# A decoder layer on eight cores: token-major residual, engines ordered by a list scheduler, and the two token mixers run side by side

## The chip, the cores and the metric

One Trainium2 chip, eight cores (two dies of four: cores 0 to 3 and 4 to 7). Each core runs the whole program on one batch element of 2048 tokens; nothing passes between the cores. The time is the device time of the slowest core, in microseconds (us). Some executions of any kernel here fall into a second, slower state, in which the cores of one die show a lower granted TensorE clock than the others. Those runs are marked slow.

Engines are named as in the profile: PE is TensorE's matmuls, PEld its weight loads, DVE VectorE, ACT ScalarE, POOL GpSimd, SP the queue that issues plain transfers.

## The reference, cut to what matters

```python
x = x + 0.5 * swiglu(rmsnorm(x), w1, w3, w2)            # D 1024, inner width 2816
h = rmsnorm(x)
u = h @ w_in                                            # q | k | v | ret gate | lru x | lru gate
# mixer A: retention, 4 heads (dk 128, dv 256), chunks of 128
ret   = retention_chunkwise(rotary(q), rotary(k), v)    # scan over 16 chunks
y_ret = (silu(g_ret) * head_groupnorm(ret)) @ w_ret_o
# mixer B: causal conv of 4 taps and a gated linear recurrence (RG-LRU), width 1024
xc = conv(x_lru)
r, i = sigmoid(xc @ w_rgate + b), sigmoid(xc @ w_igate + b)   # 8 blocks of 128
a  = exp(-8 * r * softplus(-lam))
h_t = a_t * h_{t-1} + sqrt(1 - a_t**2) * i_t * xc_t           # over time
y_lru = (h_t * gelu(g_lru)) @ w_lru_o
gates = sigmoid(h @ w_branch_gate + b)
x = x + (gates[:D] * y_ret + gates[D:] * y_lru) @ w_out
x = x + cross_attention(rmsnorm(x), rmsnorm(mem))       # 4 heads, 256 memory tokens
x = x + 0.5 * swiglu(rmsnorm(x), ...)
return rmsnorm(x)
```

The two mixers need only `h`, not each other. That is what the change uses.

## The kernel before

Operations are recorded in program order with what they read and write; each engine keeps that order, and semaphores are placed from the dependences. The mixers are two functions, called one after the other:

```python
lru_branch()
retention_branch()
mixer_tail()                     # merge projections, gates, output projection
```

The LRU works in units of one 128-channel block and half of the time axis (16 units). Every array has two sets, one for each half:

```python
def Bb(u):
    cc, hf = divmod(u, 2)
    S = sets[hf]
    # ... (tt = ii * tt on VectorE)
    if hf == 0:
        P.add("dve", lambda e: e.tensor_tensor_scan(hl.ap, ra.ap, tt_.ap, 0.0, ALU.mult, ALU.add), ...)
        P.add("dve", lambda e: e.tensor_copy(small[:, 24:25], hl.ap[:, TH - 1:TH]), reads=hl.hs, writes=[hcar])
    else:
        P.add("dve", lambda e: e.tensor_tensor_scan(hl.ap, ra.ap, tt_.ap, small[:, 24:25], ALU.mult, ALU.add), ...)
    P.add("pool", lambda e: e.tensor_tensor(BT[cc].ap[...], hl.ap, gg.ap, ALU.mult), ...)

A(0)
A2(0)
for u in range(NU):              # A: projections and conv; A2: gates; Bk_: exponentials; Bb: scan
    if u + 1 < NU:
        A(u + 1)
    Bk_(u)
    if u + 1 < NU:
        A2(u + 1)
    Bb(u)
```

In the merge, one weight tile serves four token blocks, so all eight PSUM banks fill before the first is emptied:

```python
for k in range(KC):
    for tb in range(NTB):
        ins = e.matmul(banks[bb[tb]][:, :], wt_[:, k, :], rhs_list(k, tb), start=(k == 0), stop=(k == KC - 1))
```

The softmax here doesn't subtract the row's maximum and nothing guards it: scores larger than these inputs give would overflow.

## Time and profile before

| | before |
|---|---|
| median (range) of 4 runs | 2755.9 us (2751.8 to 2759.6) |
| profiled core | core 3, 2769.7 us (an execution of its own) |
| TensorE busy, first feed-forward | 463 of 479 us, granted clock 0.98 |
| LRU alone, retention alone | 338 and 491 us, clock 0.67 and 0.78 |
| merge | 331 us |

The slices, windows, chain and groups behind this table are in the prediction, with what is to be seen in each. One reading to keep in mind: the window table gives, for each stretch of time, each engine's busy us with the number of instructions in brackets, then the granted TensorE clock as a share of full speed, the busy share of the DMA engines and their GB/s.

### The profile page before, as it was taken

What the parts mean: (1) busy time and instruction counts of PE and PEld (TensorE: products, weight loads), DVE (VectorE), ACT (ScalarE), POOL (GpSimd) and SP (SyncE); (2) the same over time, 40 slices, a digit from 0 to 9 for tenths busy, and PEclk for the clock granted to TensorE, in tenths of its full rate; (3) what the DMA queues carried; (4) which work ended last, traced back from release to release, by engine and by line L of the source; (5) the groups of instructions that cost most, each with busy time, mean ns of one, the idle gap of its engine ahead of it and who ended that gap; (6) DMA issues with size and microseconds to landing.
All of it is one profiled execution on the core that took longest, in us unless ns stands there. A gap on an engine that the chain in (4) does not pass through costs nothing.

```text
span 2769.7 us, 26087 instructions; the slowest of 8 cores (2732.2 to 2769.7 us)
## 1 busy us (share of the span) xinstructions
PE 2034.4 (73%) x8717; PEld 899.3 (32%) x8717; DVE 801.2 (29%) x1491; ACT 760.2 (27%) x1566; POOL 412.3 (15%) x441
## 2 busy tenths in 40 slices
PE   2599999965445545757576678877489699999993
PEld 2244444421111212323233233323234244444442
DVE  1313233143333352323233111112412423132333
ACT  1310100125677632333325111110323410101014
POOL 0000000001222234434343312210000000000000
PEclk9799999977667667878688888888799799999995
DMA  8022212051010033030300423333231202132103
GB/s 190 0 33 36 39 20 42 16 149 12 8 16 8 8 31 31 1 31 1 31 1 1 40 21 31 31 127 64 56 59 21 48 0 47 22 58 38 20 1 122
DMA packets 120851, 104.48 MB, mean 38 GB/s; under 512 B 78496, under 2 KB 103184, under 8 KB 118672
## 3 DMA queue, kind: packets, MB, share of 16 engines
q0 software_dynamic: 112880, 66.59, 18.1%
q1 hardware_dynamic: 7840, 36.24, 3.6%
q8 instruction: 71, 1.16, 0.2%
q14 instruction: 60, 0.49, 0.1%
HBM read 152.63 MB, written 16.78 MB: 61 GB/s over the span
## 4 chain that ended last, share of the span: by engine, by line
PE 69%; ACT 12%; DVE 6%; DMA 5%; issue 5%; POOL 2%; ACTq 0%; DVEq 0%; POOLq 0%; SPq 0%
PE bank L428 22%; PE bank L454 11%; PE bank L1181 10%; PE bank L1029 5%; PE bank L808 5%; PE bank L995 3%; PE bank L689 2%; ACT R L363 2%; PE bank L1214 2%; PE bank L614 2%; PE bank L370 2%; DMA ring<-w_in 2%; PE bank L844 1%; DVE R L499 1%; DMA R<-x 1%
## 5 line engine op out<-in xcount | busy, mean ns | idle before, releaser
L428 PE MATMUL bank<-R,ring 128*128 128x512 bf16 x2816 | 613.5, 381 | 14.3 <-DVE R L382 14.3
L428 PEld LDWEIGHTS bank<-R,ring 128*128 128x128 bf16 x2816 | 276.4, 98 | 351.3 <-issue 22.1
L454 PE MATMUL bank<-R,ring 128*128 128x512 bf16 x1408 | 313.6, 386 | 24.6 <-DVE R L437 24.6
L1181 PE MATMUL bank<-R,ring 128*128 128x512 bf16 x1024 | 263.1, 425 | 62.5 <-DVE R L1191 31.2
L434 ACT ACTIVATE R<-bank 128x512 f32<-128x512 f32 x176 | 90.9, 604 | 750.3 <-PE bank L428 750.3
L437 DVE TENSOR_TENSOR R<-bank,R 128x512 bf16<-128x512 f32 x176 | 109.2, 682 | 509.7 <-PE bank L428 509.7
L459 DVE SCALAR_TENSOR_TENSOR R<-bank,R 128x512 f32<-128x512 f32 x256 | 158.9, 682 | 178.8 <-PE bank L454 178.8
L454 PEld LDWEIGHTS bank<-R,ring 128*128 128x128 bf16 x1408 | 139.3, 99 | 198.9 <-issue 39.6
L1181 PEld LDWEIGHTS bank<-R,ring 128*128 128x128 bf16 x1024 | 108.4, 107 | 217.0 <-issue 122.8
L280 POOL DMA_DIRECT2D ring<-ffn_w x24 | 20.9, 874 | 1037.5 <-PE bank L428 611.1
L1029 PE MATMUL bank<-ring,R 128*128 128x512 bf16 x512 | 166.0, 483 | 0.1
L844 PE MATMUL bank<-R,wgate 128*128 128x512 bf16 x64 | 29.8, 621 | 175.5 <-ACT R L837 175.5
L995 PE MATMUL bank<-R,ring 128*128 128x512 bf16 x512 | 127.9, 417 | 28.9 <-DMA ring<-w_in 27.3
L808 PE MATMUL bank<-R,ring 128*128 128x512 bf16 x512 | 142.1, 447 | 0.0
L370 PE MATMUL bank<-R,onesb 128*128 128x512 bf16 x128 | 53.2, 591 | 95.8 <-ACT R L363 95.8
L829 DVE SCALAR_TENSOR_TENSOR R<-R,pc 128x1024 f32<-128x1024 f32 x48 | 61.6, 1284 | 191.0 <-ACT R L825 187.7
L1067 PE MATMUL bank<-R 128*128 128x256 bf16 x64 | 18.8, 294 | 121.8 <-ACT R L1062 116.5
L382 DVE SCALAR_TENSOR_TENSOR R<-R,pc,bank 128x512 bf16<-128x512 f32 x128 | 85.7, 741 | 72.4 <-ACT bank L379 72.4
L363 ACT ACTIVATE R<-R 128x512 bf16<-128x512 f32 x128 | 68.8, 618 | 76.0 <-DVE R L1219 76.0
L995 PEld LDWEIGHTS bank<-R,ring 128*128 128x128 bf16 x512 | 53.4, 105 | 102.4 <-issue 61.5
L808 PEld LDWEIGHTS bank<-R,ring 128*128 128x128 bf16 x512 | 58.0, 113 | 86.4 <-issue 66.0
L1029 PEld LDWEIGHTS bank<-ring,R 128*128 128x128 bf16 x512 | 59.7, 117 | 75.5 <-issue 47.9
(190 smaller groups left out, 2025.1 us busy)
## 6 DMA issues: line engine op xcount, KB each, us to landing
ring<-ffn_w POOLq DMA_DIRECT2D x12, 1536.0 KB, 12.7
ring<-ffn_w POOLq DMA_DIRECT2D x12, 1280.0 KB, 10.1
R<-x SPq DMA_DIRECT2D x16, 512.0 KB
park<-R SPq DMA_DIRECT2D x8, 1024.0 KB
R<-park SPq DMA_DIRECT2D x8, 1024.0 KB
out<-R SPq DMA_DIRECT2D x16, 512.0 KB
ring<-w_in POOLq DMA_DIRECT2D x24, 256.0 KB, 4.4
ring<-w_in POOLq DMA_DIRECT2D x8, 512.0 KB, 6.3
```

The source lines that it names most:

```text
L363: P.add("act", lambda e, c=c, tb=tb: e.activation(sq[c].ap, xT[(c, tb)].ap, AF.Square), reads=xT[(c, tb)].hs, writes=sq[c].hs)
L370: ins = e.matmul(banks[b][:, :], onesb[:, :], sq[c].ap, start=(c == 0), stop=(c == KC - 1))
L382: P.add("dve", lambda e, c=c, tb=tb, b=b: e.scalar_tensor_tensor(hT[(c, tb)].ap, xT[(c, tb)].ap, pcol(gname, c), banks[b][:, :], ALU.mult, ...
L428: ins = e.matmul(banks[bb[tb]][:, :], wtile[:, k, m * 128:(m + 1) * 128], hT[(k, tb)].ap, start=(k == 0), stop=(k == KC - 1))
L434: P.add("act", lambda e, tb=tb, ba=ba: e.activation(ssb[tb].ap, banks[ba[tb]][:, :], AF.Silu), reads=[hbk[ba[tb]]], writes=ssb[tb].hs)
L437: P.add("dve", lambda e, tb=tb, bb_=bb_, m=m: e.tensor_tensor(hid[(m, tb)].ap, banks[bb_[tb]][:, :], ssb[tb].ap, ALU.mult), reads=[hbk[bb_ ...
L454: ins = e.matmul(banks[bb[tb]][:, :], w2t[:, m, oc * 128:(oc + 1) * 128], hid[(m, tb)].ap, start=(m == 0), stop=(m == G - 1))
L459: P.add("dve", lambda e, tb=tb, bb=bb, oc=oc: e.scalar_tensor_tensor(xT[(oc, tb)].ap, banks[bb[tb]][:, :], 0.5, xT[(oc, tb)].ap, ALU.mult, ...
L808: ins = e.matmul(banks[bb[j]][:, :], wl_t[:, k, r, :], hT[(k, tbs[j])].ap, start=(k == 0), stop=(k == KC - 1))
L995: ins = e.matmul(banks[b][:, :], wt_[:, k, :], hT[(k, tb)].ap, start=(k == 0), stop=(k == KC - 1))
L1029: ins = e.matmul(banks[b][:, :], hT_all.ap[:, k, cols], wvg_t[:, k, :, :].rearrange("p r f -> p (r f)"), start=(k == 0), stop=(k == KC - 1))
L1181: ins = e.matmul(banks[bb[tb]][:, :], wt_[:, k, :], rhs_list(k, tb), start=(k == 0), stop=(k == KC - 1))
```

## The change

The intent: fill TensorE between the two feed-forward blocks. The residual is kept token-major (norms become row operations), the retention state is summed in PSUM, the memory projections are folded into the query and output weights, and LRU units and retention steps are emitted in turn. A list scheduler then lays every engine's instructions out from assumed durations. The core of the diff, cut:

```diff
-        if stage not in (23, 25, 26):
-            lru_branch()
-        retention_branch()
-        mixer_tail()
+        ret_load(0)
+        unit = lru_units()
+        ret_load(1)
+        step = ret_steps()
+        for s in range(16):
+            unit(s)
+            step(s // 8, s % 8)
+        tail()
 ...
+TAB_NS = 1283.0
+TAB_HOLD = 1200.0
 ...
+            if e == "act":
+                for (k, c, op) in a:
+                    pen = TAB_NS + TAB_HOLD if (op.tab is not None and tab[0] is not None and tab[0] not in op.tab) else 0.0
+                    cand = (t + pen, k, c, op)
 ...
+            xc = XC.v((u % 2) * 1024, 1024)
+            xcb = XCB.v()
+            tr = TR.v((u % 2) * 1024, 1024)
+            ti = TI.v()
+            mu = MU.v()
+            gg = GG.v((u % 2) * 1024, 1024)
 ...
-                P.add("dve", lambda e: e.tensor_copy(small[:, 24:25], hl.ap[:, TH - 1:TH]), reads=hl.hs, writes=[hcar])
+            prev = XC.v(((u + 1) % 2) * 1024 + 1023, 1)
 ...
+                dve(lambda e: e.tensor_tensor_scan(xc.ap, tr.ap, mu.ap, prev.ap, ALU.mult, ALU.add),
+                    tr.hs + mu.hs + prev.hs, xc.hs, 1024, 2.1)
 ...
-                    for k in range(KC):
-                        for tb in range(NTB):
-                            ins = e.matmul(banks[bb[tb]][:, :], wt_[:, k, :], rhs_list(k, tb), start=(k == 0), stop=(k == KC - 1))
+                    mm_group(banks[by][:, :], by, [(w.ap[:, 2 * br, k, :], sv[k].ap) for k in range(KC)], w.hs + hs)
+                    bg = bk.next()
+                    mm_group(banks[bg][:, :], bg, [(w.ap[:, 2 * br + 1, k, :], hT(tb, k).ap) for k in range(KC)], w.hs + hhs(tb))
```

TI, MU and XCB have one buffer each.

## The prediction

> **What bounds the kernel now.** I read the page's slices first, then cut the span into its stages by busy time and clock, then the chain that ended last, then the groups of instructions. Core 3, profiled at 2769.7 us, is the slowest of eight; the cores lie within 1.4% and no die lags, so this is a fast run.
>
> ```profile
> PE   2599999965445545757576678877489699999993
> ACT  1310100125677632333325111110323410101014
> PEclk9799999977667667878688888888799799999995
> ```
>
> These are tenths in 40 slices. TensorE is full in the two feed-forward blocks (slices 3 to 8 and 33 to 39) and at 4 to 8 tenths between them, where its granted clock is lower too. ScalarE leads only in the recurrent-unit stage.
>
> ```profile
> core 3: us, PE busy (x) PEld busy (x) DVE busy (x) ACT busy (x) POOL busy (x), PEclk, DMA share, GB/s
> 113.00:592.00 479.00, 463.45 (x2112) 207.91 (x2112) 134.26 (x219) 46.73 (x89) 7.82 (x9) 0.98 0.21 42
> 647.00:985.00 338.00, 161.46 (x544) 61.66 (x544) 116.03 (x86) 239.30 (x273) 79.72 (x42) 0.67 0.10 10
> 1045.00:1536.00 491.00, 313.43 (x1356) 140.05 (x1354) 145.38 (x560) 176.29 (x638) 206.28 (x271) 0.78 0.14 14
> 1536.00:1867.00 331.00, 263.46 (x1026) 108.49 (x1026) 39.72 (x64) 40.48 (x67) 65.31 (x63) 0.84 0.33 50
> ```
>
> In order: first feed-forward, the LRU branch alone, the retention branch alone, the merge projections. The same table gives the rest: start and first norm 113 us, mixer norm 55, rotary tables and first weights 60, output projection with the return of the residual 79, attention norm and memory keys and values 74, attention 164, norm 37, second feed-forward 477, transposes and store 72. Together 2770. Only 956 us are feed-forward; the other 1814 us hold about half of all matmuls.
>
> ```profile
> 244.53 82.89 PE bank L428 x384
> 1640.62 16.72 PE bank L1181 x64
> 1869.04 16.93 DMA ring<-w_out
> ```
>
> From the chain of waits (start, length, work). 82.89/384 = 0.216 us for a full-width matmul at full clock: this is my unit. The merge projections take 16.72/64 = 0.261 each, because every block of 64 follows a wait of about 4 us for VectorE to free banks and starts slow. The third line is a weight load that nothing covers.
>
> ```profile
> L459 DVE SCALAR_TENSOR_TENSOR R<-bank,R 128x512 f32<-128x512 f32 x256 | 158.9, 682 | 178.8 <-PE bank L454 178.8
> L829 DVE SCALAR_TENSOR_TENSOR R<-R,pc 128x1024 f32<-128x1024 f32 x48 | 61.6, 1284 | 191.0 <-ACT R L825 187.7
> L860 ACT ACT_TABLE_LOAD x16 | 20.5, 1283 | 0.3
> L862 ACT ACTIVATE R<-R,small 128x1024 f32<-128x1024 f32 x16 | 18.4, 1149 | 1.5
> PE bank L844 <- ACT R L837: 175.5, 16, 11.2
> ```
>
> These are prices (mean ns after the bar) and, last, the wait table's verdict on the LRU stage: TensorE stands 175.5 us of 338 behind one ScalarE instruction. The retention stage has the same shape with shorter waits.
>
> **What the Trainium skill says.** "TensorE: Matmul & The Clock Gate", Part 1, has a cold array at half clock until some 3.4 us of sustained work, N/1.2 against N/2.4 + 2.5 ns per matmul: 427 and 216 ns at 512 columns. The trace agrees: after a gap, weight loads of the merge projections are 0.43 us apart for about 14 matmuls, later 0.21. The same part warns of a limiter at 13/16 clock once three cores of a die run dense matmuls. The trace disagrees for the feed-forward (0.96 to 1.00 on all eight cores over stretches of 40 to 90 us), but 0.262 us spacing, which is 13/16, does show after the slow start of some LRU blocks. "ScalarE: Activation LUTs", What ACT_TABLE_LOAD costs, gives 1283 ns; the trace has 1283. Its section on table sets advises grouping by set; the kernel before loads three tables per LRU unit (48 in all).
>
> **The change, part by part.** Weights, head count and mathematics stay; layout, order and overlap change. I counted the built program's instructions and read their order on each engine. I price them with the durations above.
>
> *Start.* Ten small parameter loads one after another, f32 transposes and four ones-matmul norms (113 us) give way to a token-major norm (Square with accumulation, one scale, eight bf16 transposes per tile). TensorE's order has nearly all 16 tiles' transposes ahead of the dense part, so it waits for the whole of x. Before, 3 x 1.5 MB of bf16 weights, 9.4 MB of f32 read, arrived in 36 us and x alone at 8.4 MB in 25 us, say 260 to 335 GB/s. Here 8.9 MB share that with weights: about 58 us, and 5 for the last norm: 63, or 50 saved.
>
> *First feed-forward.* Its 2112 matmuls are the same: 456 us. Added inside are the memory keys, values and their folding into the query and output weights (192 half-width and 32 full-width matmuls, 28 us), 8 us of transposes for the next norm, and my estimate of 20 us for side loads that come late and for VectorE, which in the last group has two residual updates (0.68 each), a 1.28 scaling and half of a 1.0 copy per 2.2 us of matmuls. I put 512 against 479, but the 55 us norm after it goes.
>
> *Mixer.* The shifted q and k weights fall away (256 matmuls), state lives in PSUM, LRU and retention run together. TensorE at full clock: 576 + 256 + 512 full-width matmuls = 1344 x 0.216 = 290, small ones (256 at 128 columns, 184 at 256) 35: 325 us. ScalarE: an LRU unit is four copies or gelus (0.60), four gates (0.69), four 1024-wide passes (about 1.2): 10.0 us, x16 = 160; a retention step 6.8, x16 = 109; table switches, 22 in the built order, 28: 297. VectorE: LRU 8.25 x 16 = 132, rotary 96 x 0.69 = 66, masks and per-chunk statistics and scaling 103: 301. So three engines are nearly level, and perfect overlap would give some 330. But the order on TensorE shows that retention is served first: after its last matmul six of the 16 LRU units are still to come. Hence two parts. While both run (10 units, all of retention): TensorE 78 + 166 + 35 = 279, VectorE 251, ScalarE 222; at 85% TensorE occupancy 328. Then six units alone, ScalarE-bound: 10.0 + two table loads 2.6 + 2 for single buffers = 14.5 each: 87. With 10 for filling: 425 against 338 + 60 + 491 = 889.
>
> *Merge and output.* 1024 x 0.216 = 221 + 3, as banks now turn over per 16 matmuls, 3.5 us, against 0.69 + 0.68 of evacuation: 107 saved. Output 256 x 0.216 = 55 + 7 transposes + 3, the residual's reload running beside it: 65 against 79 + the norm part of 74.
>
> *Attention.* Query and output projections go into the folded matrices: 256 + 32 + 256 = 544 matmuls instead of 672: 118 + 7 transposes + 5 = 130, against 164 + 37, the memory part having left.
>
> *Second feed-forward, end.* 456 + 9 = 465. The last tile is already token-major: square, scale, 0.5 MB store, about 14 against 72.
>
> Sum: 63 + 512 + 425 + 224 + 65 + 130 + 465 + 14 = 1898. I predict 1905.
>
> **Rivals.**
> - *The clock limiter becomes the bound.* Weights now change at every matmul and the span has hardly a pause[...]. For: the 0.262 us spacing in LRU blocks. Against: retention's q/k projections, which already change weights each time, run at 29.7 us for 128, slow start included. If everything dense went to 13/16, 1400 us x 0.23 = 322 more: about 2230. I give it one in eight.
> - *ScalarE and the LRU chain hold the mixer.* The static order was made with assumed durations; TensorE, in order, may sit behind a late gate. Then the mixer is nearer 500 and the whole 1980. For: one pass costs DVE, POOL, PE and ACT in turn, and several buffers are single. Against: retention fills the gaps.
> - *Late side loads in the first feed-forward.* Sixteen memory jobs reuse two weight slots, each a 0.5 MB load that the trace lands in 4 to 6 us; a 3 us stall each would make 50 us: 1940.
> - *Everything overlaps as ordered*, 85% becomes 95%, and stalls vanish: about 1840.
>
> **Range and chances.** Downward I see 60 us, upward 80 from stalls and more from the clock, so 1840 to 2020. More than 840 us of the saving comes from idle time that is visible in the profile, and even the limiter case is 19% faster; being within 2% or slower would need a fault that I can't see: 0.98, 0.01, 0.01.
>
> **What would show it.** Feed-forward blocks of about 500 and 465 us at clock near 1.0, with 0.216 us per matmul (a 0.26 spacing there means the limiter); mixer near 425, of which the last 80 to 90 with TensorE under 60% and two table loads per unit; merge and output at 285 without 4 us gaps; no stage of norms; first dense matmul near 63 us. The prediction is wrong if the mixer exceeds 500, if the granted clock in the feed-forwards is near 0.8, or if TensorE waits for loads in the first one for over 40 us.

## The result, and the profile after

| | before | after |
|---|---|---|
| median of 4 runs | 2755.9 us | 2069.3 us |
| range | 2751.8 to 2759.6 | 2068.5 to 2070.0, and one slow run of 2249.5 |
| ratio of the fast runs | | 0.7509 (95%: 0.7497 to 0.7521) |

A ratio is the mean time of one kernel's fast runs over the mean of the other's fast runs in the same rounds, so it is not quite the ratio of the medians that are quoted.

The kernel is faster by a quarter, but 164 us longer than predicted, and outside the range of 1840 to 2020. The slices of the changed kernel, on its slowest core (core 5, 2068.1 us), in tenths:

```profile
PE   2599999999988877777554499999999999999997
ACT  3311121111335353535444431113544111111122
PEclk9699999999998989889766799999999999999999
```

TensorE is full from slice 3 on, except for slices 12 to 23: there it falls to 8, 7, 5 and 4 tenths and the clock falls with it. ScalarE stays at 3 to 5 tenths in the same place, so it isn't the full engine either. The stages from the first to the merge, as windows:

```profile
core 5: us, PE busy (x) PEld busy (x) DVE busy (x) ACT busy (x) POOL busy (x), PEclk, DMA share, GB/s
0.00:85.00 85.00, 21.56 (x150) 13.98 (x151) 28.55 (x60) 31.11 (x52) 25.33 (x45) 0.77 0.97 214
85.00:610.00 525.00, 501.92 (x2483) 235.04 (x2482) 218.03 (x345) 97.07 (x164) 49.41 (x92) 0.99 0.42 80
610.00:1036.00 426.00, 318.82 (x1550) 146.31 (x1547) 270.25 (x436) 202.32 (x333) 175.65 (x131) 0.88 0.09 24
1036.00:1183.00 147.00, 66.01 (x214) 23.38 (x214) 53.90 (x40) 69.17 (x80) 34.24 (x19) 0.67 0.04 7
1183.00:1406.00 223.00, 222.88 (x1027) 100.82 (x1028) 49.48 (x66) 52.35 (x72) 59.79 (x59) 0.99 0.28 49
```

In order: start, first feed-forward, mixers side by side, LRU units left over, merge. In the fourth line no engine is busy for half of the time: the engines wait for one another. Against the prediction's sum:

| stage | predicted | measured | difference |
|---|---|---|---|
| start | 63 | 85 | +22 |
| first feed-forward | 512 | 525 | +13 |
| mixers side by side (with 10 for filling) | 338 | 426 | +88 |
| LRU units left over | 87 | 147 | +60 |
| merge | 224 | 223 | -1 |
| output projection | 65 | 75 | +10 |
| attention | 130 | 129 | -1 |
| second feed-forward, end | 479 | 458 | -21 |
| sum | 1898 | 2068 | +170 |

Seven eighths of the miss is the mixer. From the chain of waits (start, length, work), the lines that answer to those of before:

```profile
1289.98 116.13 PE bank L505 x538
1406.14 19.39 DMA X<-park
1602.30 358.10 PE bank L505 x1658
```

In the merge 116.13/538 is 0.216 us a matmul where before had 0.261: the waits for banks are gone. The second line is the residual's reload, which the prediction had beside other work; TensorE is busy for 71.8 of the 75 us of the output stage all the same. The third is the second feed-forward at 358.10/1658 = 0.216 us. From the groups (line, engine, operation, tiles, count; busy us, mean ns of one; idle time before it):

```profile
L737 DVE SCALAR_TENSOR_TENSOR X<-bank,X 128x512 f32<-128x512 f32 x256 | 176.2, 691 | 111.6 <-PE bank L505 111.3
L521 ACT ACT_TABLE_LOAD x27 | 34.6, 1283 | 39.4 <-PE bank L505 30.7 <-DMA X<-x 8.4
```

Residual updates and table loads cost what before's cost (682 and 1283 ns). These prices were right; VectorE's work in the mixer, 343 us busy against 301 priced, was underpriced, and e5 below shows one reason. What was wrong in the main is in the wait table of the stretch 1036 to 1183 (engine, line, what it waited for; us in all, times, longest):

```profile
PE bank L505 <- POOL XCB L939: 57.7, 6, 20.4
PE bank L505 <- ACT TI L521: 17.9, 3, 17.5
PE bank L505 <- ACT TR L521: 14.1, 10, 4.6
```

Six waits of up to 20 us for XCB, the bf16 copy of the conv's result. Selected lines of the timeline around the longest of them (start, length, engine, line, operation, tiles; in brackets the idle time before it and what ended it):

```profile
1084.64 0.60 ACT L521 ACTIVATE XL<-bank 128x512 f32<-128x512 f32 x1 [1.91 <-PE bank L505]
1094.99 2.34 POOL L958 TENSOR_TENSOR MU<-TI,MU 128x1024 f32<-128x1024 f32 x1 [12.15 <-ACT MU L521]
1097.43 2.35 DVE L963 TENSOR_TENSOR_SCAN XC<-TR,XC,MU 128x1024 f32<-128x1024 f32 x1 [16.80 <-POOL MU L958]
1099.89 2.92 DVE L933 TENSOR_SCALAR XC<-XL,pc 128x1024 f32<-128x1024 f32 x1
1107.12 1.04 POOL L939 CAST XCB<-XC 128x1024 bf16<-128x1024 f32 x1 [4.85 <-DVE XC L936]
1108.30 1.01 PE L505 MATMUL bank<-XCB,wgate 128*128 128x512 bf16 x2 [20.36 <-POOL XCB L939]
```

The input of the next unit's conv (XL) is complete at 1085.24, but the conv (L933) starts at 1099.89, right after the scan (L963): the scan reads the old state from the array that the conv is to overwrite. VectorE stands idle for 16.80 us before the scan, and TensorE for 20.36 us. Two units take 1058.6 to 1112.6, 54 us.

The start's 22 us have at least two parts. Selected lines of its timeline, on the same core (JUNK<-X and JUNK<-MST are the sums of squares of a tile of x and of a memory tile, HB<-X the scaling of a tile of x before its transposes):

```profile
68.73 1.06 ACT L521 ACTIVATE JUNK<-X 128x1024 bf16<-128x1024 f32 x1 [2.35 <-DMA X<-x]
73.94 3.16 PE L505 MATMUL bank<-hT,W_45 128*128 128x512 bf16 x8
81.06 1.06 ACT L521 ACTIVATE JUNK<-MST 128x1024 bf16<-128x1024 f32 x1 [8.07 <-DMA MST<-mem]
82.31 0.15 DVE L641 TENSOR_SCALAR stat<-stat 128x1 f32<-128x1 f32 x1 [8.39 <-ACT JUNK L521]
83.08 1.28 DVE L650 SCALAR_TENSOR_TENSOR HB<-X,stat,ROW 128x1024 bf16<-128x1024 f32 x1
```

The last tile of x has landed by 68.73, against 58 in the prediction. But its scaling stands in VectorE's queue behind the statistics of the first memory tile, which lands only at 81; so it runs at 83.08, and its transposes at 84.51. This is queue order again: a tile for a side job holds the main path for some 7 us (an estimate: the x tile before it took 8.8 us from its sum of squares at 64.32 to its transposes at 73.13).

### The profile page after: what moved, and what is told of

Same layout as the page of the kernel before. It is cut to its first block, busy times and chain, and to the rows that moved or that the text cites. A ratio compares the mean times of both kernels' runs of the same rounds, so it can differ in the third digit from the quotient of the medians.

```text
span 2068.1 us, 24090 instructions; the slowest of 8 cores (2053.9 to 2068.1 us)
## 1 busy us (share of the span) xinstructions
PE 1776.2 (86%) x8584; PEld 815.4 (39%) x8584; DVE 904.4 (44%) x1354; ACT 615.8 (30%) x964; POOL 395.7 (19%) x435
## 4 chain that ended last, share of the span: by engine, by line
PE 70%; DVE 8%; DMA 6%; ACT 6%; issue 5%; POOL 2%; SPq 2%; DVEq 0%; ACTq 0%; POOLq 0%
PE bank L505 68%; DMA MST<-mem 2%; SPq L531 2%; ACT MU L521 2%; DVE XC L936 1%; ACT TR L521 1%; DMA XW<-w_xo 1%; POOL MU L958 1%; ACT L521 1%; DVE XC L933 1%; DMA X<-park 1%; PE bank L658 1%; DVE XC L963 1%; DMA XW<-w_xqT 1%; DMA rope<-RT 1%
## 5 line engine op out<-in xcount | busy, mean ns | idle before, releaser
L505 PE MATMUL bank<-hT,W_45 128*128 128x512 bf16 x2816 | 626.4, 382 | 2.3 <-ACT STMP L521 2.3
L505 PEld LDWEIGHTS bank<-hT,W_45 128*128 128x128 bf16 x2816 | 277.0, 99 | 333.4 <-issue 12.5
L505 PE MATMUL bank<-W_46,HID 128*128 128x512 bf16 x1408 | 314.2, 379 | 3.2 <-DVE stat L641 1.8
L719 DVE TENSOR_TENSOR HID<-bank,STMP 128x512 bf16<-128x512 f32 x176 | 121.7, 691 | 440.8 <-PE bank L505 439.1
L521 ACT ACTIVATE STMP<-bank 128x512 f32<-128x512 f32 x176 | 104.8, 596 | 686.0 <-PE bank L505 685.9
L737 DVE SCALAR_TENSOR_TENSOR X<-bank,X 128x512 f32<-128x512 f32 x256 | 176.2, 691 | 111.6 <-PE bank L505 111.3
L505 PEld LDWEIGHTS bank<-W_46,HID 128*128 128x128 bf16 x1408 | 131.8, 97 | 174.2 <-issue 29.6
L505 PE MATMUL bank<-hT,LW 128*128 128x512 bf16 x512 | 128.1, 412 | 22.9 <-ACT TI L521 22.6
L505 PE MATMUL bank<-hT,TW 128*128 128x512 bf16 x512 | 121.9, 382 | 0.0
L505 PE MATMUL bank<-RW_76,hT 128*128 128x512 bf16 x256 | 72.3, 437 | 22.4 <-DVE T_87 L1000 13.5
L505 PE MATMUL bank<-RW_75,hT 128*128 128x512 bf16 x256 | 69.4, 421 | 21.9 <-DVE T_87 L1000 10.4
L534 POOL DMA_DIRECT2D W_45<-f_w x44 | 24.4, 555 | 327.9 <-PE bank L505 327.4
```

The lines of the kernel that those rows point to most:

```text
L505: ins = e.matmul(out_ap, l, r, start=(start and i == 0), stop=(stop and i == n - 1), skip_group_check=skip)
L521: P.add("act", lambda e: e.activation(out, in_, func, **kw), reads=reads, writes=writes, cost=act_cost(n, nap), tab=tab)
L534: P.add("pool", lambda e: e.dma_start(out=out, in_=in_), reads=reads, writes=writes, cost=900, dma=nbytes)
L719: dve(lambda e: e.tensor_tensor(hd.ap, banks[b3][:, :], s.ap, ALU.mult), [hbk[b3]] + s.hs, hd.hs, TB)
L737: dve(lambda e, b=b, xv=xv: e.scalar_tensor_tensor(xv.ap, banks[b][:, :], 0.5, xv.ap, ALU.mult, ALU.add), [hbk[b]] + xv.hs, xv.hs, 512)
```

## The experiments

Two times mark the mixer in every run: the first LRU projection matmul and the first matmul of h with a merge weight. In the changed kernel these are 586.8 and 1183.3, so 596.5 us. The stretch begins inside the last 20 us of the first feed-forward; on this yardstick the prediction's 425 us are about 448. In all the full kernels the part from the first output-projection matmul to the end takes 659 to 663 us and the merge 220 to 231 (250 on the core of e2 whose clock was low in it, 223 on others), so nearly all that moves is start and mixer. The five jobs (e1 to e4, e5 to e8, e9 to e12, e13 to e16, e17 and e18) each ran the kernel before again, with medians of 2758 to 2773 us; across jobs it is the ratios that are to be compared.

| run | fast runs, us | ratio to before (95%) | mixer, us | clock in the mixer | longest TensorE wait there, us |
|---|---|---|---|---|---|
| changed kernel | 2068.5 to 2070.0 | 0.7509 (0.7497 to 0.7521) | 596.5 | 0.83 | 20.4 |
| e1 carry cell | 2007.5 to 2015.6 | 0.7291 (0.7272 to 0.7310) | 536.2 | 0.88 | 17.5 |
| e2 table hold 0 | 1997.9 to 2020.1 | 0.7244 (0.7227 to 0.7261) | 526.5 | 0.86 | 8.8 |
| e3 both | 1937.0 to 1940.6 | 0.7025 (0.7011 to 0.7040) | 463.6 | 0.97 | 3.4 |
| e4 start | 2041.8 and 2058.2 | 0.7429 (0.7383 to 0.7475) | 597.5 | 0.84 | 20.7 |
| e5 = e3, products on VectorE | 1940.4 to 1954.1 | 0.7058 (0.7009 to 0.7107) | 464.8 | 0.90 | 4.7 |
| e6 = e3, second MU | 1909.2 to 1912.2 | 0.6927 (0.6908 to 0.6947) | 438.5 | 0.96 | 3.1 |
| e7 = e3, LRU two ahead | 1996.7 and 1997.5 | 0.7239 (0.7213 to 0.7265) | 525.3 | 0.89 | 4.0 |
| e8 = e3 and e4 | 1932.8 to 1934.9 | 0.7010 (0.6991 to 0.7029) | 463.9 | 0.97 | 2.7 |
| e9 = e6, second rotary pair | 1945.9 to 1951.6 | 0.7057 (0.7020 to 0.7094) | 475.3 | 0.93 | 6.1 |
| e13 = e6's buffers, e3's order | 1938.5 to 1942.4 | 0.7036 (0.7018 to 0.7053) | 457.9 | 0.98 | 3.2 |
| e14 = e9's buffers, e6's order | 1895.3 to 1901.7 | 0.6881 (0.6864 to 0.6899) | 425.4 | 0.96 | 3.2 |
| e15 = e3, second TI, second rotary pair | 1907.8 to 1912.1 | 0.6923 (0.6907 to 0.6938) | 432.9 | 0.95 | 3.8 |
| e16 = e6 and e4 | 1876.3 to 1882.7 | 0.6811 (0.6794 to 0.6829) | 435.7 | 0.95 | 3.6 |
| e17 = e1 in the changed kernel's order | 2064.2 to 2068.0 | 0.7482 (0.7465 to 0.7499) | 592.2 | 0.83 | 20.3 |
| e18 = e14's buffers, e16's order | 1868.4 to 1872.0 | 0.6773 (0.6744 to 0.6802) | 426.1 | 0.97 | 2.9 |

All of these give correct results. e10 to e12 are wrong on purpose and stand further down.

### e1, e2, e3: the carry and the table hold

The theory: the scan's read of the other XC buffer ties the units in pairs, and the table hold puts the LRU's exponentials back so far that units are left over at the end. The rival: VectorE and GpSimd slow each other, and neither edit changes that.

```diff
 # e1
+    carry = fixed("carry", 16, F32)
-            prev = XC.v(((u + 1) % 2) * 1024 + 1023, 1)
+            prev = View(carry.ap[:, 0:1], carry.hs)
 ...     # after the first half's scan
+                dve(lambda e: e.tensor_copy(prev.ap, xc.ap[:, 1023:1024]), xc.hs, prev.hs, 1)
 # e2
-TAB_HOLD = 1200.0
+TAB_HOLD = 0.0
 # e3: both
```

> Edit: the scan's end value goes to a small cell of its own, so the next unit's convolution no longer waits for the scan that still reads the old buffer. Theory 'carry' (the unit pair is serial because of that buffer): after the last retention matmul the order now has 4 units instead of 6 to 7, and a pair takes about 36 us there instead of 54, so the stretch of LRU alone falls from 147 us to about 75 and the whole from 2069 to about 1995. Theory 'table hold' (units wait for the scheduler's reluctance to switch ScalarE's tables): exponentials are still held back, so no more than 20 us: about 2050. Theory 'contention' (VectorE and GpSimd slow each other): 2069, unchanged.

> Edit: one constant of the list scheduler, the extra 1200 ns that a table switch has to be worth, set to 0; the same instructions in another order. Theory 'table hold': the exponentials of a unit run some 20 to 40 us earlier, the LRU keeps pace with retention (the order has 1 unit of projections after the last retention matmul instead of 7), the stretch of LRU alone falls from 147 to 40 us, the shared part grows by about 20: near 1985. Theory 'carry': the pair stays serial, so the units cannot come faster than one per 27 us; 16 of them in 430 us just fit, so this too allows 1990 to 2030. Theory 'contention': 2069, or worse as more VectorE and GpSimd work falls into the shared part.

> Both edits. If the two causes are separate links of one chain, no LRU unit is left at the end (the order says so) and the mixer becomes the shared part alone, about 450 us instead of 573: 1945. If either alone is the cause, this equals the better of the two single edits within 10 us. If contention or the clock sets the shared part, it lengthens by what the units bring, some 60 us, and the gain stops at 2000.

Measured: the ratio falls from 0.7509 to 0.7291, 0.7244 and 0.7025, which is 60, 73 and 133 us of before's 2756. The two gains add, and nearly all of it is in the mixer: 60, 70 and 133 us shorter. By the medians e1 gained 57 us where its theory said 74, e2's 1999.6 us lie in the range of 'carry' (1990 to 2030) and 15 over the 1985 of 'table hold', and e3's 1939.7 are close to the 1945 expected. The rival theory of contention, for which e1 should have changed nothing, doesn't explain this part. Of the LRU units' projections, the built order of the changed kernel leaves 7 behind the last retention projection, e1's leaves 4, e2's 1, e3's none. Together the edits take away 133 of the 148 us by which the mixer had missed.

Part of this is clock. The same mixer matmuls keep TensorE busy for 405.8 us in the changed kernel, at 0.83 of the clock, and for 361.4 us in e13 (e3's order with nearly all records there), at 0.98. So about 44 us of the mixer are not idle time but longer busy time at the lower clock. After the 20 us wait shown above, the weight loads from 1112.99 to 1115.98 us follow each other at 0.43 us, twice the 0.216 of full clock. The last two columns of the table go together: where TensorE never waits longer than 3.8 us the mixer's clock is 0.95 or more, and with waits of 4.0 us and longer it is 0.93 or less.

### e4: the start

The weight slots that the first matmuls don't need, the LRU gate weights and the first side loads wait for the last tile of x:

```diff
+                    if self.which == 0 and 3 <= a < 9:
+                        late(o)          # o depends on the last load of x
 ...
-    f1.pump(3)
-    for tt in range(4, 8):
+    for tt in range(4, 16):
         load_x(tt)
+    f1.pump(3)
     f1.pump(6)
-    for tt in range(8, 16):
-        load_x(tt)
```

> Edit: weight slots 3 to 8 of the first feed-forward, all but its first second-layer slots, the gate weights and the first memory weights are loaded only once the last tile of x has landed. The start is a matter of transfer bandwidth (18 MB at 214 GB/s before the dense part): if x has the queues nearly alone, 8.9 + 1.6 MB take about 50 us and the first feed-forward begins at 60 instead of 85 us: 20 to 25 us less, about 2046. Rival: TensorE then waits for the postponed weights and gains nothing, 2069, or the norm's chain on ScalarE, VectorE and GpSimd sets the start, 2060.

Measured: the first LRU projection starts at 557.3 instead of 586.8, 29.5 us earlier; the mixer stays at 597.5. Three of five runs were slow and one of the two fast ones had two cores at 0.93 instead of 0.94 to 0.95, so the time is known only roughly: 2041.8 us where all cores agree. Up to the last x tile the start is the transfers: the first window line above has the DMA engines at 0.97 and 214 GB/s. In e4 the memory tile no longer comes late either: ScalarE reads it at 50.74, right after the last x tile at 47.86. How the 29.5 us divide between the two was not tried. 8.12 MB of the 18.17 MB landed there came over the GpSimd queue, whose weights are read as f32 and stored as bf16; counted as read that is an estimated 26 MB in 85 us, 309 GB/s. The rate was in the range that the prediction had taken (260 to 335); the bytes ahead of the last x tile were not.

### e5: products from GpSimd to VectorE

```diff
-            pool(lambda e: e.tensor_tensor(mu.ap, ti.ap, mu.ap, ALU.mult), ti.hs + mu.hs, mu.hs, pool_cost(1024))
+            dve(lambda e: e.tensor_tensor(mu.ap, ti.ap, mu.ap, ALU.mult), ti.hs + mu.hs, mu.hs, 1024)
-            pool(lambda e: e.tensor_tensor(bt.ap, xc.ap, gg.ap, ALU.mult), xc.hs + gg.hs, bt.hs, pool_cost(1024))
+            dve(lambda e: e.tensor_tensor(bt.ap, xc.ap, gg.ap, ALU.mult), xc.hs + gg.hs, bt.hs, 1024)
```

> On top of e3 (carry cell and table hold 0, 1939.7 us, 463 us from the first LRU projection matmul to the first merge matmul) the two 128x1024 products of each LRU unit (mu = ti*mu and bt = xc*gg) go from GpSimd to VectorE. In e3's mixer the same VectorE instruction takes 2.64 us (the product behind the input gate, 1024 columns) beside a GpSimd product and about 1.3 us alone, the scan 3.26 against 2.35, the conv steps 1.52 against 1.28. If VectorE and GpSimd slow each other (contention theory): those means fall to about 1.3, 2.35 and 1.3, VectorE's busy time in the mixer stays about level (+41 us of products, -36 us of slowdown), each unit's chain is 2 us shorter in the products and up to 2 us in the slowdown: mixer about 430 us, time about 1905. If the durations are only what they are (no contention), VectorE gets 41 us busier and holds the loop: mixer 470 to 500, time 1945 to 1975. If the order of the instructions holds the loop, about 1940.

The groups of VectorE in the mixer of e3:

```profile
L954 DVE SCALAR_TENSOR_TENSOR TI<-TI,XC 128x1024 f32<-128x1024 f32 x15 | 39.7, 2644 | 1.7 <-ACT TI L522 1.7
L962 DVE TENSOR_TENSOR_SCAN XC<-TR,MU 128x1024 f32<-128x1024 f32 x7 | 22.8, 3262 | 9.0 <-POOL MU L959 9.0
```

and of e5:

```profile
L954 DVE SCALAR_TENSOR_TENSOR TI<-TI,XC 128x1024 f32<-128x1024 f32 x15 | 18.9, 1262 | 4.4 <-ACT TI L522 4.1
L962 DVE TENSOR_TENSOR_SCAN XC<-TR,MU 128x1024 f32<-128x1024 f32 x7 | 16.9, 2418 | 0.2
```

The durations fell as the contention theory said, from 2.64 to 1.26 and from 3.26 to 2.42 us: VectorE is slowed by GpSimd. The time did not fall: 464.8 us of mixer against 463.6. So the contention theory had the durations right and the time wrong; the time is that of the third theory, that the order holds the loop. In e5 TensorE waits up to 4.7 us and its clock in the mixer is 0.90, so it is busy for 380 us instead of 361; whether the products, now 36 us of VectorE (19.0 and 17.0), or the new order brought these waits was not tried. The Trainium skill, "SBUF — State Buffer", Who interferes with whom, has a VectorE instruction with two SBUF inputs and a GpSimd instruction that reads SBUF block each other for a whole instruction. The trace agrees: both instructions shown have two SBUF inputs; without the GpSimd products the first takes half as long and the second a quarter less.

### e6, e7: a second MU buffer, and LRU units two ahead

```diff
 # e6
-    MU = A.buf("MU", o_, F32, 1024)
+    MU = A.buf("MU", o_, F32, 2 * 1024)
-            mu = MU.v()
+            mu = MU.v((u % 2) * 1024, 1024)
-    GG = A.buf("GG", o_, F32, 2 * 1024)
+    GG = A.buf("GG", o_, BF16, 2 * 1024)
 # e7 (on e3)
+        for s in range(2):
+            unit(s)
         for s in range(16):
-            unit(s)
+            if s + 2 < 16:
+                unit(s + 2)
             step(s // 8, s % 8)
```

> On top of e3: a second MU buffer (room made by keeping the GELU half GG in bf16). If the single MU buffer ties unit u+1's exponentials to the scan of unit u and so holds the LRU chain (28.5 us a unit in e3), the mixer falls from 463 to about 440 us and the time to about 1915. If the chain is held by the order of the instructions, by the slowed VectorE or by TensorE instead, the time stays at 1930 to 1945.

> On top of e3: the LRU units are emitted two ahead of the retention steps, so that they come first where both are ready; the built order has 21 table loads' worth of switches in place of 37. If ScalarE's table loads (1.28 us each on the LRU chain) and the LRU's place in the order hold the mixer: 16 x 1.28 = 20 us less, mixer about 440 us, time about 1915 to 1920. If it is the length of the unit's chain itself, 1935 to 1945; if later exponentials cost more than the loads save, slower, up to 1970.

e6 gained 27 us, as expected of a buffer that held the chain; e13 below shows that this reading was wrong. e7 has 16 table loads in the mixer window where e3 has 30, and lost 59 us, more than any theory allowed: fewer loads alone bring nothing (the order changed with them). TensorE now waits 35 us for the scaled copies of v on ScalarE and 28 us for the silu product on VectorE, since LRU work goes first on both.

### e8: carry, table hold and start together

> e3 and e4 together: carry cell, table hold 0, and the start's weight and side loads behind the last x tile. The start is bound by the transfers and the mixer is not touched by it, so the gains should add: 1939.7 less the 25 to 29 us that e4 gained in its fast runs, about 1913. If the delayed loads push a wait into FFN1, 1925 or more.

The edit is e1, e2 and e4 in one. It gained only 5 us. On cores 0, 1, 6 and 7 the spans are 1894 to 1907 us, against 1924 to 1938 in e3, so the start's 30 us are there. On cores 2 to 5 they are 1919 to 1933. The window table of core 3:

```profile
85.00:240.00 155.00, 155.00 (x658) 70.84 (x657) 60.58 (x104) 22.94 (x38) 12.70 (x23) 0.82 0.42 68
240.00:585.00 345.00, 329.84 (x1593) 150.78 (x1592) 126.57 (x187) 60.01 (x101) 32.57 (x60) 0.99 0.46 83
```

and of core 6, in the same execution:

```profile
85.00:240.00 155.00, 152.35 (x783) 75.81 (x781) 64.68 (x110) 28.89 (x49) 18.02 (x33) 1.00 0.51 81
```

Core 3 is never idle but does 658 matmuls where core 6 does 783. Its clock is 0.82 in this stretch and 0.99 afterwards; in slices of 20 us between 80 and 200 it is 0.81 throughout. Cores 2, 4 and 5 show the same 0.82. A stretch of 155 us at 0.82 loses an estimated 28 us, about the missing gain. In each of the three fast runs two or four cores have a mean clock of 0.967 to 0.972 and the others 0.982 to 0.986, so this is no single accident; yet in e16 and e18, with the same start, no fast run falls into two such groups (0.972 to 0.986 throughout). The record has it once more: in e2's profile cores 2 and 3 have 0.81 from 1130 to 1250 us, in the merge, where the other six have 1.00, and all eight have 1.00 from 1300 on. What triggers it is open.

### e9: a second rotary pair

```diff
-    T12 = A.buf("T12", o_, F32, 2 * TB)
+    T12 = A.buf("T12", o_, BF16, 4 * TB)
-                t1 = T12.v(0, TB)
-                t2 = T12.v(TB, TB)
+                t1 = T12.v((i % 2) * 2 * TB, TB)
+                t2 = T12.v((i % 2) * 2 * TB + TB, TB)
```

> On top of e6 (carry cell, table hold 0, second MU buffer: 1912 us, 438 us from the first LRU projection matmul to the first merge matmul): the two rotary products T12 are kept in bf16 and so get a second pair of buffers. In e6 TensorE waits 31.2 us for the VectorE product L1002 that frees a bank, behind the single T12 pair. If that pair holds TensorE: 20 to 25 us less, mixer about 415 us, time about 1888. If VectorE is simply behind (339 us busy of 438), the wait only moves: 1905 to 1915.

It lost 36 us, which neither theory allowed. A second buffer only takes waits away; so the order that the scheduler built must have been worse. That was the new theory: the order decides, and the buffers act through it.

### e10, e11, e12: each mixer alone

```diff
 # e10 (changed kernel), e11 (with e1's carry cell): constants for the retention's outputs
         for s in range(16):
             unit(s)
-            step(s // 8, s % 8)
 # e12 (changed kernel): constants for the LRU's outputs
-            unit(s)
             step(s // 8, s % 8)
```

> The changed kernel without its 16 retention steps (their outputs are set to a constant, so the result is wrong on purpose). Measures the LRU chain by itself, as the built kernel has it. The prediction took 14.5 us a unit when alone: 16 x 14.5 = 232 us from the first LRU projection matmul to the first merge matmul. If the scan's reading of the other XC buffer ties units in pairs (54 us a pair in the tail of the changed kernel's mixer), 16 x 27 = 430 us.

> As e10, with the carry cell (wrong result on purpose as well). If the carry alone ties the units: 14.5 to 20 us a unit, 232 to 320 us. If the single TI, MU and XCB buffers and the table loads hold a unit at what e3 shows (28.5 us), 430 to 456 us and no difference to e10.

> The changed kernel without its 16 LRU units (outputs constant, wrong result on purpose). The retention's TensorE work is about 768 x 0.216 = 166 us of projections and some 30 us of small matmuls. At the prediction's 85% that is 230 us from the first retention projection matmul to the first merge matmul. If retention by itself is held by its own waits (rotary buffer, silu buffer, VectorE chain), 270 to 330 us: then the shared part was not slowed by the LRU alone.

e10 takes 426.2 us from the first LRU projection to the first merge matmul, 26.6 us a unit; e11 327.4, 20.5 a unit; e12, from the first retention projection, 305.6 us (586.1 to 891.7). TensorE's wait table, e10 first:

```profile
PE bank L505 <- POOL XCB L939: 177.7, 16, 20.4
PE bank L505 <- ACT TR L521: 51.7, 31, 4.6
```

then e11:

```profile
PE bank L506 <- POOL XCB L940: 62.8, 16, 4.1
PE bank L506 <- ACT TR L522: 68.7, 31, 4.8
```

With nothing beside it, the LRU chain of the changed kernel takes about as long as the prediction had for both mixers together, and the carry cell takes 99 us off it. But e11's 20.5 us is still well over the 14.5 that the prediction had. (In e11 the scheduler built a new order too, so the 99 us are cell and order together.) The retention alone needs 306 us with TensorE busy for 241 of them: it has waits of its own, 47.4 us of them for the rotary product.

### e13, e14: the buffer without the order, and the order kept

In these kernels each engine's instructions are taken from a list written into the kernel, so buffer and order can be changed apart.

```diff
-        order = self.schedule()
+        order = self.fixed_order()       # e13: e6's buffers in e3's order; e14: e9's buffers in e6's order
```

> e6's buffers (second MU buffer, GELU half in bf16), but with every engine's instructions in e3's order (written into the kernel; two single swaps of neighbours on ScalarE and VectorE were needed where the moved buffers would deadlock). If the second MU buffer itself gave e6's 27 us, this runs in about 1912 us; if the new order that the scheduler built for it gave them, it runs as e3 does, 1935 to 1940 us.

> e9's buffers (second rotary pair in bf16 on top of e6), but in e6's order. It only takes waits away from e6, so if the order was what lost 35 us in e9 it is at or below e6's 1912 us; if the 31 us that TensorE waits in e6 for the product L1002 come from the single pair, about 1885 to 1890 us; if they come from VectorE being behind in its order, 1905 to 1912 us. If a bf16 pair is itself slow, 1945 us as e9.

e13 takes as long as e3: in this order the second MU buffer by itself is worth nothing, and e6's 27 us came with the order that the scheduler laid out once the buffer was there. e14 has e9's very buffers and takes 1898.4 us where e9 takes 1947.5: 49 us from the order alone. Against e6, in the same order, e14 gains 13 us by the ratios: this much is the second rotary pair, with the change to bf16 that made room for it.

### e15: other buffers, another order

```diff
-    TI = A.buf("TI", o_, F32, 1024)
+    TI = A.buf("TI", o_, F32, 2 * 1024)
 # and e9's T12, e6's GG
```

> On top of e3: a second TI buffer in place of e6's second MU buffer, and the second rotary pair in bf16, in the order that the scheduler builds for them. If such buffers are worth what e6 showed, 1895 to 1915 us; if the order decides, anywhere between 1905 and 1950 us.

1907.8 to 1912.1 us lies in the ranges of both theories, so it tells nothing apart.

### e16: e6 and the start

> e6 and the start of e4 together. On cores with the undisturbed clock 1912 - 29 = about 1883 us; if four cores again get 0.81 of the clock for the first 160 us of their dense matmuls, those lose 160 x 0.19 = 30 us and the run takes about 1910 us, no gain.

Measured 1878.8 us, 33 us under e6 by the medians: the first LRU projection is at 555.1 instead of 585.8, and cores 0 and 4 have a clock of 0.99 from 85 to 240 us. The start's gain is real where the clock holds.

### e17: the carry cell in the changed kernel's order

```diff
-        order = self.schedule()
+        order = self.fixed_order()       # the changed kernel's, each copy behind its scan
```

> The changed kernel with the carry cell, but with every engine's instructions in the changed kernel's own order (the eight copies follow their scans). If the read of the other XC buffer costs its 57 us (e1) as a wait on data, this runs in about 2012 us. If it costs them through the order that the scheduler built around it (the next unit's conv behind the scan in VectorE's queue), nothing is gained: 2066 to 2072 us.

Measured 2065.8 us, ratio 0.7482 against 0.7509: 7 us of the 60 that e1 gained, and by the two intervals hardly clear of noise. The wait on data is gone from the program and the time stays, because VectorE's queue still has the next unit's conv (here L1033) behind the scan:

```profile
1096.41 2.35 DVE L1064 TENSOR_TENSOR_SCAN XC<-TR,carry,MU 128x1024 f32<-128x1024 f32 x1 [14.14 <-POOL MU L1058]
1098.68 0.79 DVE L1033 TENSOR_SCALAR XC<-XL,pc 128x1024 f32<-128x1024 f32 x1
```

The Trainium skill, "TensorE: Matmul & The Clock Gate", Architectural detail, calls the queues of ScalarE and VectorE strict FIFO (first in, first out); the run agrees.

### e18: what was gained, together

The edit is e14's buffers, e4's start and e16's order.

> e14's buffers and the start of e16, in e16's order. e14 gained 14 us on e6 and e16 33 us; both in different stages, so 1912 - 14 - 33 = about 1865 us. If four cores get the 0.81 clock in FFN1 as in e8, about 1895 us.

Measured 1870.7 us (median of four, one of them slow), ratio 0.6773. It is faster than the kernel before and the changed one (199 us under the latter), and 8 us under e16. The gains add to within 6 us, and no fast run shows e8's clock.

## Why the prediction was wrong

**The step that failed is the mixer, and in it two terms.** "Then six units alone, ScalarE-bound: 10.0 + two table loads 2.6 + 2 for single buffers = 14.5 each: 87." The stretch took 147 us, and e10 measured the unit alone at 26.6 us. Nothing is bound by ScalarE there (69 us busy of 147). A unit is a loop of waits through all engines, and the scan that ends one is in VectorE's queue ahead of the conv that begins the next; the working added up the busiest engine's instructions instead of following that loop. With the carry cell it is 20.5 us (e11), so even without the fault the term was too small by 6 us a unit.

"at 85% TensorE occupancy 328": it was 426 us for a TensorE that was busy for 319 of them. Two reasons are shown. Its 279 us were priced at full clock, and the clock was 0.88, low as in all runs with long waits. And the order was read for what comes last (six units left over, the built order has seven projections) but not for what waits for what: the scheduler had planned around the carry and the table hold, and those two edits take 133 us off the whole mixer (e3). What is then left, 463.6 us, is near the 448 that the prediction means on this yardstick. The prediction did not see these two choices in the diff. That its total comes close without them is in part luck: in e3 no unit is left over, and the shared part alone takes the 464 us.

**Is it the missing cell or the order?** Both, one through the other. e17 shows that removing the dependence in the old order gives some 7 us; e1, where the scheduler may build anew, gives 60. e13 and e14 show the same for buffers. The same buffers in two orders differ by 49 us (e9 against e14), and which way an edit pushes the order can't be read from the edit.

**The start was mis-sized: 63 for 85.** That TensorE waits for all of x was right, but two things were missed. The term "8.9 MB share that with weights" left out how many weights go ahead: 18.2 MB landed, at the rate assumed, and the last x tile was there at 68.7 us. And the working has no wait for the memory tile, which holds the last x tile in VectorE's queue until 83.08. e4 and e16 take 29 to 33 us off by changing what is loaded first. The first feed-forward's +13 and the output's +10 stay unexplained in detail; the residual's reload, predicted to be hidden, is on the chain for 19.4 us there.

**What was right.** Merge 223 for 224 without the waits of before, attention 129 for 130, the second feed-forward and the end 458 for 479 (no stall to speak of), 0.216 us a matmul, table loads and evacuations at before's prices, no stage of norms. (The prediction's check "merge and output at 285" is not the sum of its own stages, 224 + 65 = 289; measured are 298.)

**The rivals.** The clock limiter did not hold the fast runs: their feed-forwards have a clock of 0.99. A clock of 0.81 to 0.82 in a fast run does appear, on four cores in e8 for 155 us and on two in e2. "ScalarE and the LRU chain hold the mixer" came nearest, 573 us where it said nearer 500; ScalarE was not the holder, the LRU chain was. It had been given as a reason for 1980 us, and the range was drawn with 80 us upward for stalls, which is where the size went wrong. Late side loads were no bound in the first feed-forward: TensorE idles 23 of 525 us in that stage; the one that cost time, the memory tile, did so in the start. Of the prediction's own signs of being wrong, a mixer over 500 us came true.

**Still open.** Why e5's shorter instructions bring nothing, what triggers the clock of e8 and e2, and how much lower than 425 us a better order could take the mixer.

## What to carry to other kernels

Price a stage of many engines by the loop of waits through one unit, buffers and queue order included, and only then by its busiest engine; a stage in which no engine is busy for half of the time, as here, is a sign of such a loop. Where a scheduler lays the order out, test an edit with the order held fixed as well: the edit and the new order it brings can have opposite signs. After removing a dependence look whether the queues still keep the old order: in e17 next to nothing was gained then.

## What the Trainium skill lacked or had wrong

- "TensorE: Matmul & The Clock Gate", Part 1, has the limiter take a whole die to 13/16 once three of its cores run dense matmuls, hold it while the load lasts, and advises to budget that for all-core work. Here eight cores ran the first feed-forward at 0.98 to 0.99 over 525 us. When 0.81 or 0.82 did come in a profile of a fast run, it was not on a whole die: on cores 2 to 5, two of each die, in e8 for some 155 us, and on cores 2 and 3 in e2's merge; the clock was back at 0.99 or 1.00 while the load went on. The slow runs, in which all cores of a die have a lower clock (0.84 to 0.85 in the changed kernel's), may be what the page describes; no profile of one was kept.
- The same part puts the return to the slow clock at about 3.4 us of idling. The runs agree in kind (longest wait up to 3.8 us: clock 0.95 or more; 4.0 us and longer: 0.93 or less). The page sizes the loss for matmul kernels; for a kernel with mixed waits the size here is 44 us of a mixer of 596.
- "SBUF — State Buffer", Who interferes with whom, is right on which instructions block each other (2.64 us against 1.26 for the product, 3.26 against 2.42 for the scan). What it lacks is that taking the blocking away may bring nothing: e5 did so for these two and gained nothing (464.8 against 463.6 us of mixer).
- No page that was read warns that in strict-FIFO queues with a fixed order a removed dependence may free nothing: e17 is some 7 us faster where the same edit with a new order is 60 us faster.
